# Which gate and up projections are made by seven products, and where their operand sums are traced

## The chip, the cores and the metric

The kernel runs on one core of one Trainium2 chip. The time is device microseconds from one execution of the whole program; the figure before is the median of three runs. TensorE multiplies, VectorE, ScalarE and GpSimd work elementwise, SyncE issues the transfers. In the profile's rows they are PE (PEld is its weight load), DVE, ACT, POOL and SP.

## The reference

Two layers of a decoder trunk over 512 tokens of width 1024, in f32. The part that the change touches is the feed-forward block of each layer:

```
hn = rms_norm(h, norm_ffn[i])
h = h + (jax.nn.silu(hn @ w_ffn_gate[i]) * (hn @ w_ffn_up[i])) @ w_ffn_down[i]
```

`w_ffn_gate` and `w_ffn_up` are 1024 x 2816, `w_ffn_down` 2816 x 1024. Ahead of the block stands the mixer (attention) with its output projection, behind it the layer's input embedding (`ple`), which begins with a norm of its own.

## The kernel before

Every f32 operand is cut into a high part, rounded to the matmul's format, and a low part, the rest; a product is then three matmuls (`mm3`: high x high, high x low, low x high). The cut of a weight tile is one ACT copy (`whl[:, 0]`) and one subtraction (`whl[:, 1]`) on POOL or DVE. There are five `whl` buffers, four `wraw` buffers for the raw weights as they land, and four `swtile` buffers `T`.

The norm (`norm_T`) runs over four tiles of 128 tokens. For each: ACT sums the squares (`junk`), POOL forms `msr`, `rsr` and the power, DVE scales two halves of the row (`xn`), PE transposes each half into a PSUM bank of tag "t" (two of them), ACT copies the high part to `xT`, DVE subtracts for the low part. In the feed-forward block ACT also copies the transposed half as it is to `xF`, for the operand sums.

The projections run over 11 pairs of column tiles, `fp` = 0 to 10. Pairs 0 to 5 are followed by the down projection of their part of `hidden`, then pairs 6 to 10 by the rest. In each pair the gate comes first (`wi` = 0), then the up projection (`wi` = 1). One of the two is done either

- plainly: 8 blocks of the contraction x 2 column tiles x 3 matmuls = 48 matmuls of 512 tokens into `gu`, with four weight tiles `whl`; or
- by seven products (`seven`), a scheme on 2 x 2 blocks of tokens, contraction and columns that needs seven block products instead of eight: 7 x 4 x 3 = 84 matmuls of 256 tokens into `st`, with seven `whl`, in the order 1, 7, 5, 2, 6, 4, 3. Products 1, 2 and 3 take raw blocks of the weights (low part on POOL); 7, 5, 6 and 4 take differences `T` that DVE forms (low part on DVE). Each product's result is then added into two output tiles `gs` by ACT and DVE.

On the token side products 1, 2 and 4 read `xT`; 7, 5, 6 and 3 read sums of its quarters (`Xw`, cut into `X`), which `operand_sums` makes once for each layer: four additions, four ACT copies, four subtractions of 1024 elements a partition. Before, pair 0 is plain, and in pairs 1 to 10 the gate goes by seven products and the up projection plainly. The operand sums are traced behind pair 0.

The order of the instructions on each engine is made by the tile scheduler: it goes by the order in which instructions are traced and by the offsets given with `prio` (`OFE` for evacuations, `OFN` for the norm, `KEEP` for the `xF` copies), and then each engine runs its list in that order.

Of the kernel before, what the change touches and what calls it, by code (L numbers as in the profile page):

```python
# [10 lines left out]
F32 = mybir.dt.float32  # L11
# [31 lines left out]
def hybrid_trunk_kernel(  # L43
# [18 lines left out]
    def f(ap):  # L62
        return ap.bitcast(F32)
# [43 lines left out]
    OFE, OFN, OFP = 100, 50, 200  # L107
    KEEP = 150

# [19 lines left out]
    @contextlib.contextmanager  # L129
    def prio(off):  # L130

        c = tc.cur_priority
        tc.cur_priority = c - off
        yield
        tc.cur_priority += off
# [236 lines left out]

    def norm_T(keep=None):


        g = next_gain.pop()
        xT = [[utile([P, 4, S], name=f"xT{i}{j}") for j in range(2)] for i in range(2)]
        with prio(OFN if last_act[0] else 5000):
            for tt, kh, xn in normed(g):
# [10 lines left out]
                latest["xT"] = ve.tensor_tensor(lo, pt, f(hi), op=ALU.subtract)  # L390
                if keep:
                    with prio(-KEEP):
                        se.activation(keep[kh][:, :, tt * P:(tt + 1) * P], pt, AF.Copy)

        def act(k, half, tt=None):
            t = xT[k // 4][half][:, k % 4, :]
            return t if tt is None else t[:, tt * P:(tt + 1) * P]
        return act

    def operand_sums(xact, F):  # L400


        a = [[F[kh][:, :, t * 256:(t + 1) * 256] for kh in range(2)] for t in range(2)]
        X = {}
        for n, (x, y, op) in ((7, (a[0][0], a[1][0], ALU.subtract)), (5, (a[1][0], a[1][1], ALU.add)),
                              (6, (5, a[0][0], ALU.subtract)), (3, (a[0][1], 6, ALU.subtract))):
            whole = utile([P, 4, 256], F32, name="Xw")
            F[n] = whole
            ve.tensor_tensor(whole, *(F[z] if isinstance(z, int) else z for z in (x, y)), op=op)
            X[n] = t = utile([P, 2, 4, 256], name=f"X{n}")  # L410
            se.activation(t[:, 0], whole, AF.Copy)  # L411
            ve.tensor_tensor(t[:, 1], whole, f(t[:, 0]), op=ALU.subtract)  # L412

        def left(n, half, k):
            if n in X:
                return X[n][:, half, k]
            t, kh = {1: (0, 0), 2: (0, 1), 4: (1, 1)}[n]
            return xact(4 * kh + k, half)[:, t * 256:(t + 1) * 256]
        return left
# [779 lines left out]
    def feed_forward(i, add_h, between):  # L1199
        lo_turn[0] = 2  # L1200
        F = dict(enumerate(utile([P, 4, S], F32, name=f"xF{j}") for j in range(2)))
        xact = norm_T(F)
        hidden, left = {}, None

# [3 lines left out]
        def units(fp):  # L1208
# [3 lines left out]
            def gate_done(j, t):  # L1212
                gate[j] = t
                se.activation(t, t, AF.Silu)

            def part(w, a2, ks, cols):
                for k, (hi, lo) in ks:
# [7 lines left out]
            for wi, w in enumerate((w_ffn_gate[i], w_ffn_up[i])):  # L1225
                if left and wi == 0:
                    seven(left, w, fp * 256, "ddss", gate_done)
                    continue
# [9 lines left out]
                else:  # L1238
                    part(w, accs, ws, slice(0, 512))
                if wi == 0:  # L1240
                    for j in range(2):
                        gate[j] = sg = etile("sg")
                        se.activation(sg, accs[j], AF.Silu)
            for j in range(2):
                sg = gate[j]
                ve.tensor_tensor(sg, sg, accs[j], op=ALU.mult)
                se.activation(hid[:, 0, j, :], sg, AF.Copy)
                ge.tensor_tensor(hid[:, 1, j, :], sg, f(hid[:, 0, j, :]), op=ALU.subtract)


        parts = range(0, 6), range(6, NF // 2)
        for fps in parts:
            for fp in fps:
                units(fp)
                if fp == 0:
                    left = operand_sums(xact, F)
            end = fps is parts[-1]
# [176 lines left out]
```

## Time and profile before

| | |
|---|---|
| median of three runs | 1566.41 us (1566.28, 1566.41, 1570.38) |
| the profiled execution's own time | 1570.22 us |
| its span, first to last instruction | 1568.4 us |
| PE busy | 1499.3 us, 96% of the span |
| DVE, ACT, POOL busy | 953.5, 800.1, 613.7 us |
| feed-forward pairs of layer 0 / layer 1 | from 356 us / from 1129 us of the span |

The rows further down come from one profiled execution. Times in them are from the start of its span; a row of the timeline has its start, its length, the engine, the line of the kernel, the operation, what it writes and reads, and in brackets the idle time of its engine just before it and who ended that. Matmuls are pipelined: the step from one start to the next is what one costs.

### The profile page before, as it was taken

To read this page: it belongs to the slowest core of one execution; us is meant where nothing else is said; L and a number is where in the kernel's file an instruction comes from. 1 tells how busy PE (TensorE), PEld (TensorE's weight loads), DVE (VectorE), ACT (ScalarE), POOL (GpSimd) and SP (SyncE) were. 2 spreads that over 40 slices of the span, in tenths; PEclk is the share of its full clock that TensorE was granted. 3 is DMA by queue.
4 is the path that set the end of the run, shared out by engine and by line. 5 is a ranking of instruction groups with operands and counts; after the bars stand their busy time and mean duration, and the time that the engine had idled before them with its cause. 6 is when DMAs were issued, how large, how long until landed. Compare 5 with 4: busy or idle time off the path is not lost.

```text
span 1568.4 us, 25192 instructions
## 1 busy us (share of the span) xinstructions
PE 1499.3 (96%) x9346; PEld 1307.9 (83%) x9346; DVE 953.5 (61%) x1840; ACT 800.1 (51%) x1705; POOL 613.7 (39%) x656
## 2 busy tenths in 40 slices
PE   6999999998999999999999999999889999999998
PEld 5898887877898888988988888778789888998888
DVE  6777869766763246534386878797666623654253
ACT  5476666655443234433355767586554432444343
POOL 3323455553344234432233235465434432444323
PEclk9999999999999999999999999999999999999999
DMA  5421321121333323342224131212223333334321
GB/s 174 124 73 42 82 68 34 48 94 58 104 95 99 99 85 108 108 134 68 81 69 123 55 80 44 81 28 64 71 81 95 94 121 95 94 95 132 111 68 54
DMA packets 114458, 134.70 MB, mean 86 GB/s; under 512 B 6864, under 2 KB 91936, under 8 KB 114336
## 3 DMA queue, kind: packets, MB, share of 16 engines
q1 hardware_dynamic: 114336, 133.10, 27.9%
q8 instruction: 74, 1.21, 0.3%
q14 instruction: 48, 0.39, 0.1%
HBM read 122.59 MB, written 2.10 MB: 80 GB/s over the span
## 4 chain that ended last, share of the span: by engine, by line
PE 76%; DVE 13%; ACT 4%; POOL 3%; issue 2%; DMA 1%; POOLq 0%; DVEq 0%; ACTq 0%; SPq 0%
PE acc L223 6%; PE acc L224 6%; PE acc L225 6%; PE gu L225 5%; PE gu L223 5%; PE gu L224 5%; PE st L224 4%; PE st L225 4%; PE st L223 4%; PE accr L223 2%; PE accr L224 2%; PE accr L225 2%; PE sc L866 2%; PE ge L223 2%; PE pTp L887 2%
## 5 line engine op out<-in xcount | busy, mean ns | idle before, releaser
L202 POOL TENSOR_TENSOR whl<-wraw,whl 128x512 fp32r<-128x512 f32 (+2 forms) x208 | 282.4, 1363 | 490.1 <-ACT whl L199 461.2
L199 ACT ACTIVATE whl<-wraw 128x512 fp32r<-128x512 f32 (+2 forms) x336 | 210.1, 631 | 263.6 <-PE acc L225 123.3
L202 DVE TENSOR_TENSOR whl<-wraw,whl 128x512 fp32r<-128x512 f32 x128 | 112.7, 882 | 171.7 <-ACT whl L199 171.3
L224 PE MATMUL gu<-xT,whl 128*128 128x512 f32 (+1 forms) x448 | 161.8, 362 | 0.0
L225 PE MATMUL gu<-xT,whl 128*128 128x512 f32 (+1 forms) x448 | 161.5, 362 | 0.0
L223 PE MATMUL gu<-xT,whl 128*128 128x512 f32 (+1 forms) x448 | 161.1, 361 | 0.0
L446 POOL TENSOR_TENSOR whl<-wraw,whl 128x512 fp32r<-128x512 f32 x60 | 87.1, 1452 | 153.7 <-ACT whl L445 153.6
L223 PE MATMUL acc<-whl,hid 128*128 128x512 f32 x352 | 139.1, 395 | 0.0
L224 PE MATMUL acc<-whl,hid 128*128 128x512 f32 x352 | 139.1, 395 | 0.0
L225 PE MATMUL acc<-whl,hid 128*128 128x512 f32 x352 | 138.8, 394 | 0.0
L446 DVE TENSOR_TENSOR whl<-T,whl 128x512 fp32r<-128x512 f32 x80 | 76.4, 955 | 66.2 <-ACT whl L445 65.6
L879 POOL TENSOR_SCALAR p<-p,rc,gt 128x128 f32<-128x128 f32 (+3 forms) x128 | 79.3, 630 | 71.0 <-DVE rc L877 20.8
L223 PE MATMUL st<-X,whl 128*128 128x256 f32 x320 | 91.5, 286 | 7.9 <-ACT X L411 7.9
L224 PE MATMUL st<-X,whl 128*128 128x256 f32 x320 | 92.1, 288 | 4.3 <-DVE X L412 4.3
L874 ACT ACTIVATE p<-sc,mx 128x128 f32<-128x128 f32 (+3 forms) x160 | 83.9, 535 | 22.7 <-DVE mx L871 20.6
L225 PEld LDWEIGHTS gu<-xT,whl 128*128 128x128 f32 x448 | 84.1, 188 | 13.5
L224 PEld LDWEIGHTS gu<-xT,whl 128*128 128x128 f32 x448 | 84.1, 188 | 13.0
L223 PEld LDWEIGHTS gu<-xT,whl 128*128 128x128 f32 x448 | 84.0, 188 | 12.9
L225 PE MATMUL st<-X,whl 128*128 128x256 f32 x320 | 91.4, 285 | 0.0
L445 ACT ACTIVATE whl<-T 128x512 fp32r<-128x512 f32 x80 | 50.1, 626 | 70.5 <-PE gu L225 57.4
L893 DVE TENSOR_TENSOR pT<-pTp,pT 128x512 fp32r<-128x512 f32 (+2 forms) x120 | 70.5, 596 | 19.5 <-ACT pT L892 18.5
L892 ACT ACTIVATE pT<-pTp 128x512 fp32r<-128x512 f32 (+2 forms) x120 | 62.1, 528 | 38.0 <-PE pTp L887 36.7
(334 smaller groups left out, 4499.4 us busy)
## 6 DMA issues: line engine op xcount, KB each, us to landing
wraw<-in_w_ffn_gate_dram SPq DMA_DIRECT2D x44, 512.0 KB, 3.6
wraw<-in_w_ffn_up_dram SPq DMA_DIRECT2D x44, 512.0 KB, 3.7
wraw<-in_w_ffn_down_dram SPq DMA_DIRECT2D x44, 512.0 KB, 3.8
wraw<-in_w_in_dram SPq DMA_DIRECT2D x36, 512.0 KB, 3.6
wraw<-in_w_out_dram SPq DMA_DIRECT2D x16, 512.0 KB, 3.8
wraw<-in_w_ple_gate_dram SPq DMA_DIRECT2D x16, 512.0 KB, 3.5
sw<-nq SPq DMA_DIRECT2D x32, 128.0 KB, 2.3
wraw<-in_w_in_dram SPq DMA_DIRECT2D x8, 280.0 KB, 2.9
```

The source lines that it names most:

```text
L199: se.activation(whl[:, 0], raw[:, lo:lo + n], AF.Copy)
L202: eng.tensor_tensor(whl[:, 1], raw[:, lo:lo + n], f(whl[:, 0]), op=ALU.subtract)
L223: i = te.matmul(acc, lhsT=lh, rhs=rh, start=start, stop=False, skip_group_check=True)
L224: te.matmul(acc, lhsT=lh, rhs=rl, start=False, stop=False, skip_group_check=True)
L225: te.matmul(acc, lhsT=ll, rhs=rh, start=False, stop=stop, skip_group_check=True)
L445: se.activation(whl[:, 0], src, AF.Copy)
L446: (ge if n in (1, 2, 3) else ve).tensor_tensor(whl[:, 1], src, f(whl[:, 0]), op=ALU.subtract)
L866: te.matmul(s[:, c:c + w], lhsT=lhsT, rhs=rhs, start=(j == 0), stop=False, skip_group_check=True)
L874: se.activation(e[:, u * n:(u + 1) * n], s[:, u * n:(u + 1) * n], AF.Exp, bias=mx[:, u:u + 1], accum_out=sm[:, u:u + 1])
L879: ge.tensor_scalar(e[:, u * n:(u + 1) * n], e[:, u * n:(u + 1) * n], rc[:, u:u + 1], gates[u] if gates else 1.0, op0=ALU.mult, op1=ALU.mult)
L892: se.activation(hi, src, AF.Copy)
L893: ve.tensor_tensor(lo, src, f(hi), op=ALU.subtract)
```

## The change

For `fp` of 1 or more, the projection with index `wi` goes by seven products where (2 fp + wi) is not a multiple of 3. So pair 1 has gate seven, up plain; pair 2 both seven; pair 3 gate plain, up seven; then the same again from pair 4. Of the 22 projections of a layer 13 go by seven products instead of 10. The steps behind an up projection (multiply, copy, subtract) become `up_done`, which an up projection by seven products calls for each of its two outputs.

The `xF` copies of ACT are gone. `operand_sums` adds the high and low parts of `xT` instead: two additions of 1024 elements on POOL (first 256 tokens) and two on DVE (last 256). It is traced between the gate and the up projection of pair 0.

```diff
--- before.py
+++ after.py
@@ -105,7 +105,6 @@
 
 
     OFE, OFN, OFP = 100, 50, 200
-    KEEP = 150
 
     def weave(*streams):
 
@@ -370,8 +369,7 @@
                 yield tt, kh, xn
         done.clear()
 
-    def norm_T(keep=None):
-
+    def norm_T():
 
         g = next_gain.pop()
         xT = [[utile([P, 4, S], name=f"xT{i}{j}") for j in range(2)] for i in range(2)]
@@ -388,28 +386,33 @@
                 if tt == 0 and kh == 1:
                     latest["first tile"] = last_act[0]
                 latest["xT"] = ve.tensor_tensor(lo, pt, f(hi), op=ALU.subtract)
-                if keep:
-                    with prio(-KEEP):
-                        se.activation(keep[kh][:, :, tt * P:(tt + 1) * P], pt, AF.Copy)
 
         def act(k, half, tt=None):
             t = xT[k // 4][half][:, k % 4, :]
             return t if tt is None else t[:, tt * P:(tt + 1) * P]
+        act.tiles = xT
         return act
 
-    def operand_sums(xact, F):
-
-
-        a = [[F[kh][:, :, t * 256:(t + 1) * 256] for kh in range(2)] for t in range(2)]
-        X = {}
-        for n, (x, y, op) in ((7, (a[0][0], a[1][0], ALU.subtract)), (5, (a[1][0], a[1][1], ALU.add)),
-                              (6, (5, a[0][0], ALU.subtract)), (3, (a[0][1], 6, ALU.subtract))):
-            whole = utile([P, 4, 256], F32, name="Xw")
-            F[n] = whole
-            ve.tensor_tensor(whole, *(F[z] if isinstance(z, int) else z for z in (x, y)), op=op)
-            X[n] = t = utile([P, 2, 4, 256], name=f"X{n}")
-            se.activation(t[:, 0], whole, AF.Copy)
-            ve.tensor_tensor(t[:, 1], whole, f(t[:, 0]), op=ALU.subtract)
+    def operand_sums(xact):
+
+
+        X, whole = {}, {}
+
+        for kh in range(2):
+            F = utile([P, 2, 4, 256], F32, name="xF")
+            for t in range(2):
+                hi, lo = (xact.tiles[kh][j][:, :, t * 256:(t + 1) * 256] for j in range(2))
+                whole[t, kh] = F[:, t]
+                (ve if t else ge).tensor_tensor(F[:, t], f(hi), f(lo), op=ALU.add)
+        for pair in (((7, (0, 0), (1, 0), ALU.subtract), (5, (1, 0), (1, 1), ALU.add)),
+                     ((6, 5, (0, 0), ALU.subtract), (3, (0, 1), 6, ALU.subtract))):
+            W = utile([P, 2, 4, 256], F32, name="Xw")
+            for j, (n, x, y, op) in enumerate(pair):
+                whole[n] = W[:, j]
+                ve.tensor_tensor(W[:, j], whole[x], whole[y], op=op)
+                X[n] = t = utile([P, 2, 4, 256], name=f"X{n}")
+                se.activation(t[:, 0], W[:, j], AF.Copy)
+                ve.tensor_tensor(t[:, 1], W[:, j], f(t[:, 0]), op=ALU.subtract)
 
         def left(n, half, k):
             if n in X:
@@ -1198,9 +1201,8 @@
 
     def feed_forward(i, add_h, between):
         lo_turn[0] = 2
-        F = dict(enumerate(utile([P, 4, S], F32, name=f"xF{j}") for j in range(2)))
-        xact = norm_T(F)
-        hidden, left = {}, None
+        xact = norm_T()
+        hidden, left = {}, []
 
         def hact(k, half, tt):
             return hidden[k // 2][:, half, k % 2, tt * P:(tt + 1) * P]
@@ -1212,6 +1214,12 @@
             def gate_done(j, t):
                 gate[j] = t
                 se.activation(t, t, AF.Silu)
+
+            def up_done(j, up):
+                sg = gate[j]
+                ve.tensor_tensor(sg, sg, up, op=ALU.mult)
+                se.activation(hid[:, 0, j, :], sg, AF.Copy)
+                ge.tensor_tensor(hid[:, 1, j, :], sg, f(hid[:, 0, j, :]), op=ALU.subtract)
 
             def part(w, a2, ks, cols):
                 for k, (hi, lo) in ks:
@@ -1223,8 +1231,9 @@
                             first.append(m.ins)
 
             for wi, w in enumerate((w_ffn_gate[i], w_ffn_up[i])):
-                if left and wi == 0:
-                    seven(left, w, fp * 256, "ddss", gate_done)
+
+                if fp and (2 * fp + wi) % 3:
+                    seven(left[0], w, fp * 256, ("ddss", "sott")[wi], (gate_done, up_done)[wi])
                     continue
                 accs = [bank(t, name=f"gu{wi}{j}") for j, t in enumerate(("dd", "ss" if fp == 0 else "to")[wi])]
                 ws = enumerate(weights(w, allk, fp * 256, 256, 2))
@@ -1237,23 +1246,20 @@
                         part(w, accs, ws, slice(256, 512))
                 else:
                     part(w, accs, ws, slice(0, 512))
-                if wi == 0:
-                    for j in range(2):
+                for j in range(2):
+                    if wi:
+                        up_done(j, accs[j])
+                    else:
                         gate[j] = sg = etile("sg")
                         se.activation(sg, accs[j], AF.Silu)
-            for j in range(2):
-                sg = gate[j]
-                ve.tensor_tensor(sg, sg, accs[j], op=ALU.mult)
-                se.activation(hid[:, 0, j, :], sg, AF.Copy)
-                ge.tensor_tensor(hid[:, 1, j, :], sg, f(hid[:, 0, j, :]), op=ALU.subtract)
+                if fp == 0 and wi == 0:
+                    left.append(operand_sums(xact))
 
 
         parts = range(0, 6), range(6, NF // 2)
         for fps in parts:
             for fp in fps:
                 units(fp)
-                if fp == 0:
-                    left = operand_sums(xact, F)
             end = fps is parts[-1]
             kts = list(range(2 * fps[0], 2 * fps[-1] + 2))
             for c, tags in ((0, "ddss"), (512, "stto")):
```

The rows that follow are the order of instructions on one engine, in layer 0; layer 1 has the same there. On POOL, around the norm of the feed-forward block, the kernel before has four times `msr`, `rsr` and power, one for each tile of tokens:

```order
L322 TENSOR_SCALAR msr<-ss 128x1
L335 TENSOR_TENSOR rsr<-msr,ss 128x1
L336 TENSOR_TENSOR rsr<-rsr,mhalf 128x1
L322 TENSOR_SCALAR msr<-ss 128x1
L335 TENSOR_TENSOR rsr<-msr,ss 128x1
L336 TENSOR_TENSOR rsr<-rsr,mhalf 128x1
L202 TENSOR_TENSOR whl<-wraw,whl 128x512 x2
```

These are the third and the fourth tile. In the changed kernel, same place (`xT_4407` and `xT_4408` are the high and low part of the first half of a row, `xT_4409` and `xT_4410` those of the second):

```order
L406 TENSOR_TENSOR xF<-xT_4407,xT_4408 128x1024
L321 TENSOR_SCALAR msr<-ss 128x1
L406 TENSOR_TENSOR xF<-xT_4409,xT_4410 128x1024
L334 TENSOR_TENSOR rsr<-msr,ss 128x1
L335 TENSOR_TENSOR rsr<-rsr,mhalf 128x1
L321 TENSOR_SCALAR msr<-ss 128x1
L334 TENSOR_TENSOR rsr<-msr,ss 128x1
L335 TENSOR_TENSOR rsr<-rsr,mhalf 128x1
L201 TENSOR_TENSOR whl<-wraw,whl 128x512 x2
```

Both of POOL's additions now stand ahead of the third tile's power.

On DVE, behind the last low part of `xT`, the kernel before goes on with weights, the multiplication of pair 0 (L1246) and only then the operand sums:

```order
L390 TENSOR_TENSOR xT_4412<-xnT,xT_4411 128x4x128
L202 TENSOR_TENSOR whl<-wraw,whl 128x512
L446 TENSOR_TENSOR whl<-T,whl 128x512 x2
L1246 TENSOR_TENSOR sg<-sg,gu_4632 128x512
L1246 TENSOR_TENSOR sg<-sg,gu_4633 128x512
L409 TENSOR_TENSOR Xw<-xF_4407 128x1024
L446 TENSOR_TENSOR whl<-T,whl 128x512
L409 TENSOR_TENSOR Xw<-xF_4407,xF_4408 128x1024
L462 TENSOR_TENSOR gs_4777<-part,st_4840 128x256
L412 TENSOR_TENSOR X_4754<-Xw,X_4754 128x1024
```

In the changed kernel, same place:

```order
L406 TENSOR_TENSOR xF<-xT_4407,xT_4408 128x1024
L406 TENSOR_TENSOR xF<-xT_4409,xT_4410 128x1024
L412 TENSOR_TENSOR Xw<-xF 128x1024 x2
L201 TENSOR_TENSOR whl<-wraw,whl 128x512
L415 TENSOR_TENSOR X_4630<-Xw,X_4630 128x1024
L434 TENSOR_TENSOR T<-wraw,T 128x512
L412 TENSOR_TENSOR Xw<-Xw,xF 128x1024
L415 TENSOR_TENSOR X_4634<-Xw,X_4634 128x1024
L412 TENSOR_TENSOR Xw<-xF,Xw 128x1024
L415 TENSOR_TENSOR X_4639<-Xw,X_4639 128x1024
L415 TENSOR_TENSOR X_4643<-Xw,X_4643 128x1024
L449 TENSOR_TENSOR whl<-T,whl 128x512 x2
```

All of the operand sums now stand ahead of the multiplication of pair 0 (L1220), which comes next.

On PE, 22 matmuls of pair 0 stand ahead of the third tile's transposes before; these are the last of them, the transposes, and what follows:

```order
L225 MATMUL gu_4514<-xT_4409,whl 128x256
L223 MATMUL gu_4515<-xT_4409,whl 128x256
L382 MATMUL xnT<-ident,xn 128x128 x4
L224 MATMUL gu_4515<-xT_4410,whl 128x256
L225 MATMUL gu_4515<-xT_4409,whl 128x256
```

In the changed kernel 28 of them stand ahead of these transposes, and the tile's second transposes follow one matmul later:

```order
L224 MATMUL gu_4504<-xT_4409,whl 128x256
L222 MATMUL gu_4505<-xT_4409,whl 128x256
L380 MATMUL xnT<-ident,xn 128x128 x4
L223 MATMUL gu_4505<-xT_4410,whl 128x256
L380 MATMUL xnT<-ident,xn 128x128 x4
```

Before the fourth tile's last transposes PE has 51 matmuls of pair 0 behind it in the old order, and 43 in the new. In the new order DVE also scales both halves of the third and of the fourth tile (four `xn`) ahead of the third tile's low parts.

## Rows read from the trace of the kernel before

**Rows 1.** The profile page, busy time of each engine, share, instructions

```profile
PE 1499.3 (96%) x9346; PEld 1307.9 (83%) x9346; DVE 953.5 (61%) x1840; ACT 800.1 (51%) x1705; POOL 613.7 (39%) x656
```

**Rows 2.** Busy time in four stretches: start, end, length; engines; clock, DMA

```profile
core 0: us, PE busy (x) PEld busy (x) DVE busy (x) ACT busy (x) POOL busy (x), PEclk, DMA share, GB/s
382.96:413.14 30.18, 24.18 (x134) 21.10 (x133) 24.29 (x26) 13.53 (x22) 12.80 (x8) 0.89 0.26 79
413.14:423.03 9.89, 9.89 (x85) 9.88 (x84) 6.20 (x9) 6.17 (x12) 6.05 (x5) 1.00 0.24 72
423.03:434.11 11.08, 11.08 (x51) 9.02 (x49) 7.05 (x10) 3.57 (x6) 3.90 (x3) 1.00 0.40 126
1155.75:1185.35 29.60, 23.42 (x135) 20.41 (x134) 24.59 (x26) 13.53 (x22) 12.52 (x8) 0.94 0.27 81
```

**Rows 3.** Timeline of PE: where pairs begin and where it waits for sums

```profile
382.96 0.28 PE L223 MATMUL st<-xT,whl 128*128 128x256 f32 x1
...
390.27 0.58 PE L223 MATMUL st<-X,whl 128*128 128x256 f32 x1 [3.21 <-ACT X L411]
...
400.20 0.39 PE L224 MATMUL st<-X,whl 128*128 128x256 f32 x1 [1.51 <-DVE X L412]
...
413.14 0.28 PE L223 MATMUL st<-xT,whl 128*128 128x256 f32 x1
```

**Rows 4.** Timeline of PE: transposes of the third and the fourth tile

```profile
359.81 0.63 PE L382 MATMUL xnT<-ident,xn 128*128 128x128 f32 x4 [0.81 <-DVE xn L369]
...
364.02 0.63 PE L382 MATMUL xnT<-ident,xn 128*128 128x128 f32 x4 [0.90 <-DVE xn L369]
...
365.83 0.66 PE L382 MATMUL xnT<-ident,xn 128*128 128x128 f32 x4
```

**Rows 5.** Timeline of POOL and DVE, same stretch of the norm

```profile
356.32 0.22 POOL L322 TENSOR_SCALAR msr<-ss 128x1 f32<-128x1 f32 x1 [3.55 <-ACT junk L313]
358.05 0.19 POOL L335 TENSOR_TENSOR rsr<-msr,ss 128x1 f32<-128x1 f32 x1 [1.51 <-ACT junk L313]
358.31 0.57 POOL L336 TENSOR_TENSOR rsr<-rsr,mhalf 128x1 f32<-128x1 f32 x1
...
355.33 0.68 DVE L390 TENSOR_TENSOR xT<-xnT,xT 128x512 fp32r<-128x512 f32 x1
...
358.92 0.75 DVE L369 SCALAR_TENSOR_TENSOR xn<-h,rsr,gx 128x512 f32<-128x512 f32 x1 [0.80 <-POOL rsr L336]
```

**Rows 6.** Line L202: POOL at 1024 elements, ns least/median/most

```profile
L202 POOL TENSOR_TENSOR we<-wraw,we x2: 2398/2401/2404, 679.4 to 1451.3; 128x1024 fp32r<-128x1024 f32 x2
```

**Rows 7.** Granted clock of PE (third from last) after two gaps

```profile
1016.00:1020.00 4.00, 1.68 (x10) 1.17 (x10) 4.00 (x12) 3.69 (x17) 0.35 (x1) 1.00 0.13 49
...
246.00:247.00 1.00, 1.00 (x5) 0.73 (x4) 1.00 (x6) 1.00 (x4) 1.00 (x3) 0.50 0.00 0
```

**Rows 8.** Timeline of PE: the ends of those two gaps

```profile
244.53 0.44 PE L866 MATMUL sc<-nk,nq 128*128 128x384 f32 x1 [2.30 <-ACT p L874]
...
1018.38 0.44 PE L866 MATMUL sc<-nk,nq 128*128 128x384 f32 x1 [2.32 <-ACT p L874]
```

**Rows 9.** Timeline of DVE: one operand sum alone

```profile
392.41 1.21 DVE L409 TENSOR_TENSOR Xw<-Xw,xF 128x1024 f32<-128x1024 f32 x1
```

**Rows 10.** Timeline of POOL and DVE within the seven products of pair 2

```profile
414.62 2.54 POOL L1248 TENSOR_TENSOR hid<-gs,hid 128x512 fp32r<-128x512 f32 x2 [1.98 <-ACT hid L1247]
417.15 1.72 POOL L446 TENSOR_TENSOR whl<-wraw,whl 128x512 fp32r<-128x512 f32 x1
...
414.06 0.69 DVE L446 TENSOR_TENSOR whl<-T,whl 128x512 fp32r<-128x512 f32 x1
415.89 1.83 DVE L446 TENSOR_TENSOR whl<-T,whl 128x512 fp32r<-128x512 f32 x1 [1.14 <-ACT whl L445]
417.65 0.42 DVE L460 TENSOR_TENSOR part<-part,st 128x256 f32<-128x256 f32 x1
```

## The prediction, made before the changed kernel ran

> **What bounds the kernel now.** I read the page's busy times first: PE works 96% of the span, the next engine, DVE, 61% [rows 1]. An average hides stages, so the windows came next, cut where a gate's first `st` matmul or an up projection's first `gu` matmul starts. In the settled part of the feed-forward block PE never waits: pair 2 takes 9.89 us for the gate by seven products and 11.08 us for the plain up projection, 20.97 together, at full clock [rows 2]. There only fewer or cheaper matmuls shorten anything. Pair 1 is different: the same work takes 30.18 us in layer 0 and 29.60 us in layer 1 [rows 2]. The timeline shows why: PE waits 3.21 us for the cut of an operand sum and 1.51 us for another, the largest of several waits [rows 3], DVE is busy 24.29 of 30.18 us, and the clock averages 0.89 [rows 2], since it falls to half behind the long wait. The sums are formed only behind pair 0's multiplication, when PE already wants them. Last I looked at the norm ahead of pair 0, where the change puts work on POOL: there PE waits 0.81 and 0.90 us for scaled rows [rows 4], and these wait for POOL's power (0.57 us, [rows 5]).
>
> **Six projections more by seven products.** Three more for each layer. One saves 11.08 - 9.89 = 1.19 us of PE [rows 2], if PE stays the bound: 6 x 1.19 = **7.1 us**.
>
> **Sums ahead of need.** Pair 1 loses 30.18 - 20.97 = 9.2 us in layer 0 and 29.60 - 20.97 = 8.6 us in layer 1 [rows 2], half clock included: **17.8 us**, if the sums come in time. DVE has now ten operations of 1.21 us [rows 9] (two additions for `xF`, four sums, four low parts) and four of 0.69 us [rows 10] up to the low part of pair 1's second `T`, 14.9 us. POOL's three operations on `whl` meanwhile take turns with them (see the lock below) at an estimated 1.3 us each (2.54 us for two, [rows 10]): 18.7 us. By the norm's walk below DVE starts at about 369.0, so that low part is there at 387.7 and the one before it at 387.0. PE ends pair 0 at 382.96 [rows 3] plus the norm's 2.1 us, 385.1, and a product lasts 9.89 / 7 = 1.41 us, so product 7 wants its low part at about 386.7. I put 0.4 us for each layer on it, **0.8 us**; the ends are 0 and half of the old loss, 4.5 us for each layer.
>
> **The norm's power waits behind POOL's additions.** Of 1024 elements one such operation takes POOL 2.40 us [rows 6]. The first is ready when DVE has written the second tile's first low part, 355.33 + 0.68 = 356.0 [rows 5]; it ends at 358.4; `msr` (0.22) follows; the second addition lasts to 361.0; then `rsr` (0.19) and the power (0.57) [rows 5], with some 0.1 us between them, end at 362.0. Before they ended at 358.9, so `xn` starts 3.1 us later. PE has six more matmuls of 0.12 us (9.89 / 84, [rows 2]) to do ahead of these transposes, but then waits some 3.2 us instead of 0.81. The fourth tile catches up in part: its power ends at about 364.1, DVE scales four halves until 365.6 and then writes two low parts, which free the two PSUM banks for the fourth tile's transposes, the last of them at about 367.0 instead of 365.83 [rows 4], with 43 matmuls of pair 0 done instead of 51. That is 1.2 + 8 x 0.12 = 2.1 us for each layer. A PE wait of this length can also halve the clock: behind a wait of 2.30 us [rows 8] PE ran at 0.50, the 1.2 GHz level [rows 7], for some 3.7 us, which costs half of that, 1.85 us; behind 2.32 us [rows 8] it kept 1.00 [rows 7]; behind 3.21 us [rows 3] it fell. Two of three: 1.2 us. Together 3.3 us for each layer, **6.6 us**; the ends are 0 (the additions are over before anyone asks) and 4.0 for each layer. The Trainium skill ("TensorE: Matmul & The Clock Gate", Part 1) has half rate as the state of an idle array, released by activity; by it each of the two waits would cost the whole 1.85 us, and the sum would be 1.3 us worse. One wait in rows 8 kept the clock, so I don't take it whole.
>
> ACT loses its eight `xF` copies for each layer. Two of them stand in the norm's chain, but that chain now goes through POOL, so this counts nothing.
>
> **Two projections by seven products in a row.** The twelve new neighbours: in each layer six times two such projections follow each other (pair 2; 3 and 4; 5; 6 and 7; 8; 9 and 10). PE needs 2 x 9.89 = 19.8 us for two. DVE's operations on two SBUF operands and POOL's exclude each other: the low part at 415.89 took 1.83 us instead of 0.69 and ended 0.6 us after POOL's operation that was under way, while the addition at 417.65, which reads PSUM, took its 0.42 us beside POOL [rows 10]. In two neighbours these are 16 x 0.69 on DVE and 8 x 1.3 on POOL (six low parts, one pair's two `hid`), 21.4 us, and 1.4 more where an up projection's outputs, now in SBUF, are multiplied: 1.6 to 3.0 us more than PE needs. The plain projections between have 4.0 to 8.0 us of such work in 11.08, so the average holds and only the lead counts. Five `whl` buffers let the cut run ahead: product 4 of pair 2 had its low part at 415.89 + 1.83 = 417.7 [rows 10], and PE came to it at 413.14 + 5 x 1.41 + two matmuls = 420.4, a lead of 2.7 us. So most of the excess is covered; I take 0.15 us for each of 12 places, **1.8 us**, with ends 0 and 3.0. The Trainium skill ("SBUF — State Buffer", Who interferes with whom) states the same lock, an operation of DVE with two SBUF inputs against one of POOL that reads SBUF, the later one blocked for the whole of the other; it speaks against this change, and it is the second rival below.
>
> **No cost.** ACT would be at some 14 us in 19.8 (6.17 in 9.89 with one such projection, [rows 2]) and stays short of PE. The `ple` loads move on SP from pair 0 to pair 10; their transposes stay where they were, in the last pair, and have them by then. Raw weights for a second projection in a row land during the plain one ahead of it.
>
> **Sum.** 7.1 + 17.8 - 0.8 - 6.6 - 1.8 = 15.7 us. The profiled execution's own time is 1570.22 us (span 1568.4 and 1.8 around it), so it would be 1554.5. It lies 3.8 us above the median of the three runs, of which one reads 1570.38 and two 1566.3 to 1566.4; I take the difference from the median: 1566.4 - 15.7 = **1550.7 us**, with its own range of 1546 to 1557.
>
> **Rivals.**
> First, POOL's additions cost nothing, because they are over before the third tile's sum of squares is there. For it: POOL idles 3.55 us there [rows 5]. Against: both stand ahead of the power on POOL. It gives 6.6 us more, 1544.1.
> Second, the lock becomes the bound in the twelve places, and the kernel gets slower. DVE's list is in order; an addition that waits for PE holds up the differences behind it, so the lead may not build up. Without this stall the gain is 17.5 us, so from 1.46 us for each place the gain is gone. At 2.5 us each, 30 instead of 1.8, it is 1578.9.
> Third, the change doesn't do what it says: the sums are traced early but still come late, since DVE's 18.7 us fit with nothing to spare. With half the old loss left (8.9 instead of 0.8) it is 1558.8.
>
> **How the numbers follow.** A measurement here can tell about 0.3%, 4.7 us, from no change: faster is below 1561.7, slower above 1571.1. My forecast has 0.57, the first rival 0.12, the third 0.12, the second 0.10 (a third of it between 1562 and 1571), and 0.09 is for what I don't see, a third of it on each side and between. Faster 0.57 + 0.12 + 0.12 + 0.03 = 0.84, same 0.03 + 0.03 = 0.06, slower 0.10. The range has to hold 0.8: forecast, first and third rival make 0.81, from 1541.5 (nothing lost of 24.9) to 1561.
>
> **What would show it.** Pair 1 of both layers, from its first `st` matmul to that of pair 2, should take some 21.4 us instead of 30.18 and 29.60. In the norm POOL should show two additions of about 2.4 us ahead of the third tile's power, and PE one wait of about 3.2 us for `xn`. Pairs 2, 5 and 8 should take 19.8 us each with no wait of PE; waits on `whl` there for DVE's or POOL's low part would be the second rival. The prediction is wrong if PE's waits in the feed-forward block together exceed some 10 us, or if a projection by seven products takes more than 10 us behind another.

## The result, and the profile after

The kernel after takes 1551.16 us (median of 5 runs, 1549.74 to 1553.40), the kernel before 1570.23 (median of 5, 1566.28 to 1572.16): a ratio of 0.9883, 95% interval 0.9863 to 0.9904, some 19 us faster. The forecast was 1550.7, in a range of 1541.5 to 1561. The profiled execution has a span of 1548.0 us against 1568.4. Busy times of the page after, to be read beside [rows 1]:

```profile
PE 1490.1 (96%) x9562; PEld 1313.8 (85%) x9562; DVE 1004.0 (65%) x1910; ACT 809.3 (52%) x1725; POOL 650.3 (42%) x666
```

PE has 216 matmuls more and is busy 9 us less, and its share is the same 96%. Where the time went is read from stretches cut where a pair's first matmul starts, as in [rows 2]. In this order: pair 0, pair 1 and the two neighbouring projections by seven of pair 2 (all layer 0), then pairs 0 and 1 of layer 1.

```profile
core 0: us, PE busy (x) PEld busy (x) DVE busy (x) ACT busy (x) POOL busy (x), PEclk, DMA share, GB/s
355.47:384.35 28.88, 25.15 (x209) 24.59 (x208) 24.37 (x26) 15.16 (x25) 12.98 (x11) 1.00 0.18 56
384.35:405.48 21.13, 21.13 (x135) 19.00 (x134) 14.74 (x22) 9.81 (x19) 11.59 (x8) 1.00 0.33 100
405.48:425.26 19.78, 19.78 (x170) 19.78 (x168) 14.47 (x21) 12.42 (x24) 10.88 (x8) 1.00 0.29 89
1117.42:1147.15 29.73, 26.45 (x210) 26.06 (x208) 24.39 (x26) 15.19 (x26) 12.93 (x11) 0.94 0.17 54
1147.15:1168.30 21.15, 21.15 (x135) 19.03 (x134) 14.72 (x22) 9.81 (x19) 11.66 (x8) 1.00 0.33 100
```

Pair 1 takes 21.13 and 21.15 us with PE busy throughout; it took 30.18 and 29.60 [rows 2]. Two projections by seven in a row take 19.78 us, twice 9.89. Of the pairs only pair 0 got longer: it took 26.72 and 26.68 us and takes 28.88 and 29.73. The view of waits says how, for PE from the start of pair 0 to the end of pair 10, layer 0 and layer 1 (columns: who waited for whom, us in total, times, longest):

```profile
PE xnT L380 <- DVE xn L368: 3.2, 1, 3.2
PE xnT L380 <- DVE xT L388: 0.5, 1, 0.5
...
PE xnT L380 <- DVE xn L368: 3.3, 1, 3.3
```

The view shows no other wait of PE there. None is for a sum or for a cut weight. The timeline of POOL, then of DVE, around the long wait of layer 0, against [rows 5]:

```profile
355.33 2.42 POOL L406 TENSOR_TENSOR xF<-xT,xT 128x1024 f32<-128x1024 f32 x1 [3.33 <-DVE xT L388]
357.83 0.22 POOL L321 TENSOR_SCALAR msr<-ss 128x1 f32<-128x1 f32 x1
358.13 2.36 POOL L406 TENSOR_TENSOR xF<-xT,xT 128x1024 f32<-128x1024 f32 x1
360.45 0.19 POOL L334 TENSOR_TENSOR rsr<-msr,ss 128x1 f32<-128x1 f32 x1
360.72 0.57 POOL L335 TENSOR_TENSOR rsr<-rsr,mhalf 128x1 f32<-128x1 f32 x1
...
361.32 1.41 DVE L368 SCALAR_TENSOR_TENSOR xn<-h,rsr,gx 128x512 f32<-128x512 f32 x2 [3.45 <-POOL rsr L335]
```

The power, at 358.31 before, is now at 360.72, though the whole stretch lies 0.8 us earlier in this profile; it stands behind two additions of some 2.4 us. DVE is idle for 3.45 us waiting for it, and PE waits behind DVE. From first gate matmul to the end of the second down projection, the two layers get 10.3 and 8.8 us shorter, 19.1 together; the other 1.3 of the 20.4 us by which the span shrank lie outside these blocks.

### The profile page after: what moved, and what is told of

Same layout as the page of the kernel before. It is cut to its first block, busy times and chain, and to the rows that moved or that the text cites. A ratio compares the mean times of both kernels' runs of the same rounds, so it can differ in the third digit from the quotient of the medians.

```text
span 1548.0 us, 25774 instructions
## 1 busy us (share of the span) xinstructions
PE 1490.1 (96%) x9562; PEld 1313.8 (85%) x9562; DVE 1004.0 (65%) x1910; ACT 809.3 (52%) x1725; POOL 650.3 (42%) x666
## 4 chain that ended last, share of the span: by engine, by line
PE 78%; DVE 11%; POOL 4%; ACT 3%; issue 2%; DMA 0%; POOLq 0%; ACTq 0%; DVEq 0%
PE acc L222 6%; PE acc L223 6%; PE acc L224 6%; PE st L223 6%; PE st L222 6%; PE st L224 6%; PE gu L223 4%; PE gu L224 4%; PE gu L222 4%; PE accr L222 2%; PE accr L223 2%; PE sc L869 2%; PE accr L224 2%; PE no L1086 2%; PE pTp L890 2%
## 5 line engine op out<-in xcount | busy, mean ns | idle before, releaser
L201 POOL TENSOR_TENSOR whl<-wraw,whl 128x512 fp32r<-128x512 f32 (+2 forms) x196 | 270.0, 1384 | 467.1 <-ACT whl L198 453.7
L198 ACT ACTIVATE whl<-wraw 128x512 fp32r<-128x512 f32 (+2 forms) x312 | 195.1, 631 | 254.4 <-PE acc L224 136.8
L201 DVE TENSOR_TENSOR whl<-wraw,whl 128x512 fp32r<-128x512 f32 x116 | 103.1, 891 | 171.6 <-ACT whl L198 171.3
L449 POOL TENSOR_TENSOR whl<-wraw,whl 128x512 fp32r<-128x512 f32 x78 | 116.1, 1496 | 141.5 <-ACT whl L448 139.2
L223 PE MATMUL gu<-xT,whl 128*128 128x512 f32 (+1 forms) x352 | 124.8, 355 | 0.0
L224 PE MATMUL gu<-xT,whl 128*128 128x512 f32 (+1 forms) x352 | 124.6, 355 | 0.0
L222 PE MATMUL gu<-xT,whl 128*128 128x512 f32 (+1 forms) x352 | 124.0, 354 | 0.0
L449 DVE TENSOR_TENSOR whl<-T,whl 128x512 fp32r<-128x512 f32 x104 | 102.6, 993 | 29.3 <-ACT whl L448 28.9
L223 PE MATMUL st<-X,whl 128*128 128x256 f32 x416 | 116.9, 281 | 0.0
L222 PE MATMUL st<-X,whl 128*128 128x256 f32 x416 | 116.8, 281 | 0.0
L224 PE MATMUL st<-X,whl 128*128 128x256 f32 x416 | 116.6, 280 | 0.0
L223 PE MATMUL st<-xT,whl 128*128 128x256 f32 x312 | 87.6, 281 | 0.0
L224 PE MATMUL st<-xT,whl 128*128 128x256 f32 x312 | 87.5, 280 | 0.0
L222 PE MATMUL st<-xT,whl 128*128 128x256 f32 x312 | 87.5, 280 | 0.0
L448 ACT ACTIVATE whl<-T 128x512 fp32r<-128x512 f32 x104 | 64.2, 625 | 42.8 <-PE gu L224 24.2
L896 DVE TENSOR_TENSOR pT<-pTp,pT 128x512 fp32r<-128x512 f32 (+2 forms) x120 | 70.5, 595 | 19.9 <-ACT pT L895 18.9
```

Source lines behind the costliest of these rows:

```text
L198: se.activation(whl[:, 0], raw[:, lo:lo + n], AF.Copy)
L201: eng.tensor_tensor(whl[:, 1], raw[:, lo:lo + n], f(whl[:, 0]), op=ALU.subtract)
L222: i = te.matmul(acc, lhsT=lh, rhs=rh, start=start, stop=False, skip_group_check=True)
L223: te.matmul(acc, lhsT=lh, rhs=rl, start=False, stop=False, skip_group_check=True)
L224: te.matmul(acc, lhsT=ll, rhs=rh, start=False, stop=stop, skip_group_check=True)
L448: se.activation(whl[:, 0], src, AF.Copy)
```

## Experiments

Each is the kernel after with the edit shown; e1 to e10 are short names. The kernel before ran beside them: 1571.4 us with e1 to e4, 1572.2 with e5 to e8 and 1571.2 with the last three. The figures in brackets behind a median are the lowest and the highest run, the ratio to the kernel before and its 95% interval. From the end of layer 0's feed-forward block to layer 1's pair 0 two profiles of one kernel stand up to 2.7 us apart (405.4 us in e6 and 402.7 in e9, the same kernel), so the verdicts rest on the lengths of single stretches first, and on the medians second.

**The sums without the new rule (e2).**

```diff
-                if fp and (2 * fp + wi) % 3:
+                if fp and wi == 0:
```

> The changed kernel with the old rule: gate by seven products in every pair from 1 on, up always plainly; only the place of the operand sums is new. Theory (the two parts add): 6 x 1.19 = 7.1 us more than the changed kernel, 1558.3, pair 1 at 21.1 us, every later pair at 20.97, pair 0 still at 28.9 and 29.7. Rival (the six more projections by seven products bring nothing, and all of the gain is in the place of the sums): 1551.

It took 1557.4 us (1555.1 to 1559.7; 0.9908, 0.9889 to 0.9927). Pair 1 takes 21.17 and 21.08 us, pair 0 28.82 and 30.64, and pairs 2 to 9 some 21.0 each. So some 14 us of the gain come from the early sums alone, net of the longer pair 0. The rule brings the rest: 5 to 6 us by the medians, and by the lengths of pairs 2 to 10, which are 3.5 and 3.6 us shorter in the kernel after, the 7.1 that six conversions make at 1.19 us. The 30.64 is longer than any pair 0 forecast here; the clock stands at half for 6.8 us of it (see the account of the norm below).

**The rule without the early sums (e3).**

```diff
-                if fp == 0 and wi == 0:
+                if fp == 0 and wi == 1:
```

> The changed kernel with the operand sums traced behind pair 0, as before, and the new rule for the projections. Theory: pair 1 takes some 30 us again (9 us more in each layer), pair 0 gets its 26.7 us back since POOL's additions no longer stand ahead of the power; in all 17.5 - 5.2 = 12 us more than the changed kernel, 1563.5. Rival (the place of the sums doesn't matter, since the sums are now made by DVE and POOL from the cut parts and not from ACT's copies): pair 1 stays near 21 us, 1551 or less.

It took 1575.4 us (1571.0 to 1579.2; 1.0026, 1.0014 to 1.0038), slightly slower than before, where I had expected 1563.5. Pair 0 goes to 25.88 and 26.15 us: the long wait there does come from the place of the additions. But pair 1 takes 36.8 and 36.6 us, some seven more than before. Timeline of POOL, then DVE, in pair 1:

```profile
381.55 2.40 POOL L406 TENSOR_TENSOR xF<-xT,xT 128x1024 f32<-128x1024 f32 x1
383.90 4.45 POOL L1222 TENSOR_TENSOR hid<-sg,hid 128x512 fp32r<-128x512 f32 x2
388.31 3.33 POOL L406 TENSOR_TENSOR xF<-xT,xT 128x1024 f32<-128x1024 f32 x1
...
381.84 5.38 DVE L406 TENSOR_TENSOR xF<-xT,xT 128x1024 f32<-128x1024 f32 x2
...
387.48 5.24 DVE L412 TENSOR_TENSOR Xw<-xF 128x1024 f32<-128x1024 f32 x2
```

Both engines now add side by side, each operation waiting for one of the other engine's: DVE's two additions take 5.38 us (2.35 in the kernel after) and its first two sums 5.24. PE's waits in pair 1 grow from 6.0 us before to 12.0, and the clock is at half for 13.7 us in either layer instead of 6.8 and 3.4; what share of the seven us is the clock's is not shown. Splitting the four additions over DVE and POOL saves nothing when both halves are wanted at once.

**POOL's additions behind the fourth tile's power (e1).**

```diff
-                (ve if t else ge).tensor_tensor(F[:, t], f(hi), f(lo), op=ALU.add)
+                if t:
+                    ve.tensor_tensor(F[:, t], f(hi), f(lo), op=ALU.add)
+                else:
+                    with tc.issue_after(latest["pow"].ins):
+                        ge.tensor_tensor(F[:, t], f(hi), f(lo), op=ALU.add)
```

> The changed kernel, with POOL's two additions of the operand sums held back until the fourth tile's power has been issued. Theory (the additions stand ahead of the power on POOL and so delay the norm): PE's wait of 3.2 us for xn goes, pair 0 takes 26.7 to 27.2 us again instead of 28.9 and 29.7, pair 1 stays at 21.1 because POOL is idle behind the power and DVE wants the sums only some 2 us later; about 5 us less than the changed kernel, 1546. Rival (the wait has another cause, the order of the sums of squares or of the matmuls): pair 0 stays at 29 us and the time at 1551.

It took 1556.6 us (1553.8 to 1558.9; 0.9902, 0.9884 to 0.992), and pair 0 grew to 31.14 and 32.27 us instead of shrinking. The power is early now, but look at POOL, and at DVE just after it:

```profile
364.63 0.57 POOL L335 TENSOR_TENSOR rsr<-rsr,mhalf 128x1 f32<-128x1 f32 x1
365.16 5.10 POOL L410 TENSOR_TENSOR xF<-xT,xT 128x1024 f32<-128x1024 f32 x2
...
365.23 5.58 DVE L368 SCALAR_TENSOR_TENSOR xn<-h,rsr,gx 128x512 f32<-128x512 f32 x2 [0.38 <-POOL rsr L335]
```

DVE's two scaled rows of the fourth tile, 1.41 us elsewhere, take 5.58: each comes behind one of POOL's additions, since they read two SBUF operands too. PE waits 2.52 and 2.01 us for them, and from the second wait on the clock is at half for 3.4 us in layer 0 and 6.8 in layer 1. My expectation moved the additions out of POOL's queue for the power and put them under the lock that the prediction itself had named. In the kernel after, the same additions run while DVE is idle or reads PSUM, so there the queue costs, and here the lock.

**No additions on POOL, in two ways (e7 and e6).** First all four on DVE, e7:

```diff
-                (ve if t else ge).tensor_tensor(F[:, t], f(hi), f(lo), op=ALU.add)
+                ve.tensor_tensor(F[:, t], f(hi), f(lo), op=ALU.add)
```

> The kernel after with all four additions on DVE, none on POOL. Theory (it is POOL's place ahead of the power that costs, and DVE has no room to spare before pair 1): pair 0 goes back to 26.7 to 27.7 us, but DVE carries 2.4 us more before product 7 of pair 1 while pair 1 begins some 2 us earlier, so pair 1 grows from 21.1 to 22 to 23.5 us, with a PE wait on an operand sum or a low part; the median is 1547 to 1551. Rival (the sums had room): pair 0 at 26.7 and pair 1 at 21.1, 1546. Rival (the lock between DVE and POOL has no part in it and the place ahead of the power costs nothing): pair 0 stays at 28.9 to 29.7.

Then none at all, e6, with the whole activations copied out of PSUM by ACT as in the kernel before (only the main lines are shown; the helper's additions drop out, `whole[t, kh]` is a view of `kept[kh]`):

```diff
+                if keep:
+                    with prio(-150):
+                        se.activation(keep[kh][:, tt // 2, :, tt % 2 * P:tt % 2 * P + P], pt, AF.Copy)
...
-                (ve if t else ge).tensor_tensor(F[:, t], f(hi), f(lo), op=ALU.add)
```

> The kernel after, but the four whole activations are written by ScalarE's eight copies out of PSUM, as in the kernel before, and the four additions (two on POOL, two on DVE) are gone; the sums are still traced early. Theory (POOL's additions ahead of the third tile's power make pair 0 of each layer longer): pair 0 takes 26.7 us again in both layers instead of 28.88 and 29.73, the PE wait of 3.24 and 3.28 us for scaled rows goes back to some 0.8, pair 1 stays at 21.0 (DVE has 2.4 us less to do), and the median is 1551.2 - 5.2 = 1546 us. Rival (the longer pair 0 comes from the sums of the early tracing on DVE, or the eight ACT copies cost as much where they now stand): pair 0 stays at 28.5 or more and the median at 1550 to 1553.

With the copies it took 1547.8 us (1543.2 to 1549.8; 0.9843, 0.9824 to 0.9862). Pair 0 is back at 26.72 and 26.80 us, PE's waits there are 0.83 and 0.91 (0.85 and 0.89), and pair 1 takes 20.96 and 20.99. So of all that is now traced early it is the additions that cost in the norm.

With everything on DVE it took 1551.7 us (1549.0 to 1554.1; 0.9872, 0.9856 to 0.9887), just above the range I gave and for a reason I had not foreseen: pair 1 takes 20.96 us, and pair 0 stays long, 29.84 and 30.06. PE's long wait for `xn` is gone (0.32 and 0.24 us are left), so that one was POOL's doing; but now PE waits for POOL itself. PE, POOL and DVE in that kernel:

```profile
371.01 0.58 PE L224 MATMUL gu<-xT,whl 128*128 128x256 f32 x1 [2.64 <-POOL whl L201]
...
364.64 8.03 POOL L201 TENSOR_TENSOR whl<-wraw,whl 128x512 fp32r<-128x512 f32 x2 [5.50 <-ACT whl L198]
...
362.84 2.35 DVE L406 TENSOR_TENSOR xF<-xT,xT 128x1024 f32<-128x1024 f32 x2
365.11 2.35 DVE L412 TENSOR_TENSOR Xw<-xF 128x1024 f32<-128x1024 f32 x2
367.38 0.68 DVE L201 TENSOR_TENSOR whl<-wraw,whl 128x512 fp32r<-128x512 f32 x1
367.98 1.22 DVE L415 TENSOR_TENSOR X<-Xw,X 128x1024 fp32r<-128x1024 f32 x1
```

DVE issues operations on two SBUF operands without a gap, each starting as the last one ends, and two cuts on POOL, some 1.3 us each elsewhere, take 8.03. The first alone takes 6.32: it waits through six operations of DVE (from the second `xF` to a `T` behind the rows shown) and ends behind the first pause in that row. The second takes 1.77. A loser of the lock does not always wait that long: in the kernel after two such cuts, under a row of DVE just as dense, take 1.79 and 2.35 us, so each got its turn behind one operation. What decides between the two is not shown. From PE's wait of 2.64 us on the clock is at half for 3.4 us in both layers, which is part of the longer pair 0. (Counted from the norm's first transposes, which the mixer puts 4.4 us earlier in layer 0 of this profile, pair 1 begins 3.1 and 3.3 us later than with the copies.)

**All projections of pairs 1 to 10 by seven (e4, and e8 with more load buffers).**

```diff
-                if fp and (2 * fp + wi) % 3:
+                if fp:
```

> The changed kernel with both projections of every pair from 1 on by seven products, 20 in a layer instead of 13, with no plain one between. Theory (the exclusion of DVE and POOL is the bound where no plain projection lets the lead be rebuilt): a pair takes 21.4 to 22.8 us, the sum of DVE's operations on two SBUF operands and POOL's, instead of 19.8, with PE waiting for low parts of the weights; 20 pairs at 22.1 come to some 29 us more than the changed kernel, 1580, and not below 1565. Rival (the exclusion costs nothing, PE stays the bound): pairs at 19.8 us, 14 x 1.19 = 16.7 us less than the changed kernel, 1534.5.

It took 1605.6 us (1604.3 to 1609.0; 1.0218, 1.0201 to 1.0235). A pair takes 23.8 us on average in the first half of the block and 22.7 in the second; behind the first pairs of a half it settles at some 23.8 in both, more than the 21.4 to 22.8 which I worked out for the lock, so something else was in it. DVE's waits between 395 and 490 us:

```profile
DVE T L434 <- DMA wraw<-in_w_ffn_up_dram: 12.2, 4, 3.4
DVE T L434 <- DMA wraw<-in_w_ffn_gate_dram: 10.3, 4, 3.4
DVE whl L449 <- ACT whl L448: 1.1, 4, 0.3
```

DVE waits 22.5 us for raw weights. There are four buffers of them, two for each projection by seven, and SP's queue waits for POOL to let one go: the third projection in a row loads late. So the next run, e8, gave it six buffers, and 14 instead of 15 large tiles to make room.

```diff
-        raw = wpool.tile([P, 1024], F32, name="wraw", tag="wraw", bufs=4)
+        raw = wpool.tile([P, 1024], F32, name="wraw", tag="wraw", bufs=6)
```

> All projections of pairs 1 to 10 by seven products, as in e4_all_seven, but with six buffers for raw weights instead of four (and 14 instead of 15 large tiles, to make room). Theory A (in e4_all_seven DVE waited 22.5 us for raw weights between 395 and 490 us, since SP's queue waits for a raw buffer that POOL still reads; three projections by seven in a row use up the lead of the loads): a pair takes 20 us or little more instead of 23.8 and 22.7, and the median is about 1536 to 1545 us. Theory B (the lock between DVE and POOL is the bound: 21.4 us of operations that exclude each other, and 22.8 with the multiplications on SBUF operands, against 19.8 of PE): a pair stays at 21.4 to 22.8 us with PE waiting for low parts, and the median is 1580 to 1600.

It took 1576.7 us (1572.3 to 1577.9; 1.0024, 1.0012 to 1.0035); with fewer large tiles its pair 0 takes 32.1 us, so only its later pairs are compared. Each half of either layer takes 105.0 to 105.4 us for five pairs, 21.0 for one on average. That average hides the lead: the first pair of a half takes 19.8 us and the second 19.9 to 20.4, and only from the third on does a pair settle, at some 21.6 (21.6 to 22.1). The third pair of layer 0, in the columns of [rows 2]:

```profile
435.75:457.36 21.61, 20.64 (x170) 20.06 (x169) 21.15 (x29) 11.74 (x24) 12.81 (x8) 1.00 0.33 98
```

DVE's waits for loads are gone and DVE is busy 21.15 of 21.61 us, its blocked time included: now it is the bound. So theory A explains some 2.2 us of e4's loss for each settled pair, and theory B the last 1.8. Both causes were in e4. Theory B's pair, 21.4 to 22.8 us, came out in the settled pairs; neither median did, and the longer pair 0 blurs that comparison. DVE's operations start 0.60 us apart though each row gives 0.68 or 0.69: with the two multiplications by the gate that is 18 x 0.60 + 8 x 1.3 = 21.2, an estimate in which the additions that read PSUM run beside POOL.

**One buffer of cut weights less (e5).**

```diff
-        whl = wpool.tile([P, 2, 560], F32R, name="whl", tag="whl", bufs=5)[:, :, :n]
+        whl = wpool.tile([P, 2, 560], F32R, name="whl", tag="whl", bufs=4)[:, :, :n]
```

(and the same in the helper for seven products; that line is not shown)

> The kernel after with four buffers of cut weights (whl) instead of five. My prediction covered the excess of two projections by seven in a row (21.4 to 22.8 us of DVE and POOL work against 19.8 of PE) by the lead that five buffers give, some 2.7 us. If that lead is what covers it, one buffer less takes 1.4 us of it: PE then waits in the back-to-back places of pairs 2, 3 to 4, 5, 6 to 7, 8 and 9 to 10, up to 1.4 us each, 12 places: 1556 to 1568 us. If the lead is not needed (the excess is not there, or the plain projection between carries it), nothing changes: 1551, with pair 2 at 19.8.

It took 1567.6 us (1564.8 to 1572.0; 0.9974, 0.9962 to 0.9985), within the range I gave for a needed lead, but that time says nothing on it: 16 us came from the stages that also cut weights, the mixers and pair 0 (30.90 and 31.32). In the places themselves pair 2 takes 20.12 instead of 19.78 us and pairs 3 and 4 19.90 instead of 19.81; the twelve places lose 2.6 us together, 0.05 to 0.36 each. So the fifth buffer's lead is used, but for little.

**The copies again beside the kernel after (e9), and three of four by seven (e10).** The first two runs are the kernel after unchanged and, as e9, the kernel of e6, on one chip.

> The kernel after, unchanged, beside the next two on one chip: 1551 us, pair 0 at 28.9 and 28.9 to 29.7 us.

> The same kernel as e6_act_copies, beside the kernel after on one chip. By the segments of its trace (pair 0 2.16 and 2.93 us shorter, pair 1 0.17 and 0.16) it should be 5.4 us faster than after, 1546 us; by the medians of two different chips the difference was only 3.4 us. If it is under 2 us, part of the gain is given back somewhere that the two profiles don't show.

They took 1550.2 us (1548.3 to 1553.9; 0.9866, 0.9848 to 0.9885) and 1546.9 (1542.6 to 1549.2; 0.9838, 0.9816 to 0.986): 3.3 us apart, where the feed-forward blocks of the two profiles differ by 5.6. The two intervals overlap, so the size of the gain is open between the two numbers. Then e10, the copies with three of four projections by seven:

```diff
-                if fp and (2 * fp + wi) % 3:
+                if fp and (2 * fp + wi) % 4 != 3:
```

> e6_act_copies with three of four projections by seven products in place of two of three (plain are only the up projections of pairs 1, 3, 5, 7, 9): two conversions more for each layer, 4 x 1.19 = 4.8 us less PE. Theory (the lead covers the excess of three in a row, 1.8 us at the 21.0 us for two that e8_all_seven_raw6 needed when all were by seven products): three in a row take 29.7 us, and the median is 4.8 us under e9's, about 1541. Rival (four buffers of raw weights hold only two projections by seven, so that the third loads late, as in e4_all_seven): the third takes 0.5 to 2 us more in 8 places of the two layers, PE waits there for low parts whose difference on DVE waited for a load, and the median is equal to e9's or up to 11 us above.

It took 1544.3 us (1543.6 to 1546.2; 0.9827, 0.9809 to 0.9845), the lowest median of all, 5.9 us under the kernel after beside it; its interval overlaps that of e9. Three in a row:

```profile
405.82:435.50 29.68, 29.68 (x253) 29.67 (x252) 26.84 (x34) 17.96 (x36) 19.30 (x12) 1.00 0.28 80
```

That is 3 x 9.89 without a stall, in all eight places (29.68 to 29.74), though DVE waits three times for loads in layer 0's first half, up to 2.5 us; the rival is out. At e8's settled rate three in a row would want an estimated 32.4 us, 2.7 more than PE and not the 1.8 of my expectation; that is as much as the lead of 2.7 that the prediction read from [rows 10]. But the gain on e9 is 2.6 us and not 4.8. Pairs 6 to 10, where the two conversions of a layer lie, are 2.11 and 2.01 us shorter instead of 2.38, and the second down projection behind them is 0.75 and 0.81 longer: PE idles 0.74 and 0.75 us there ahead of a transpose of `ple`, and has no such idle time in e9. By these stretches it is 2.6.

## Why the prediction was right, and where it was not

**The conversions** (7.1 us): pairs 2 to 10 are 3.44 us shorter in layer 0 and 3.66 in layer 1, 7.1.

**The sums** (17.8 less 0.8): pair 1 is 9.05 and 8.45 us shorter, 17.5. The low parts were in time to within 0.2 us (pair 1's gate takes 10.05 and 10.06 us instead of 9.89), where I had 0.4 for each layer. Timeline of DVE:

```profile
381.75 2.43 DVE L415 TENSOR_TENSOR X<-Xw,X 128x1024 fp32r<-128x1024 f32 x2
384.09 2.39 DVE L449 TENSOR_TENSOR whl<-T,whl 128x512 fp32r<-128x512 f32 x2
```

The second `T`'s low part ends at 386.5; I had said 387.7. Of these 1.2 us, 0.8 is only that the stretch lies that much earlier in this profile. DVE needs 18.4 us for the row, from 368.1 on, where I had 18.7, and two errors of mine cancel in that: an operation that is not blocked costs 1.13 us from start to start (0.60 for 512 elements), where I took its row's 1.21 (0.69), so the fourteen cost 13.7 us and not 14.9; and POOL's cuts, four and not three, hold DVE up for 4.7 us and not 3.9. The third rival (sums still late) fell here.

**The norm** (6.6): 2.16 and 3.05, 5.2. The mechanism, the place and the wait (3.24 and 3.28 us, some 3.2 forecast) came out, and 2.1 us without the clock was right: 2.16. The mis-sized term is the clock. In layer 0 PE kept the full clock behind the wait; in layer 1 the clock fell to half, 1.2 GHz, for 3.4 us; a stretch of one us within it, and pair 0 of e2's layer 1, where the same norm stands, in the columns of [rows 2] (the granted clock is third from last):

```profile
1126.00:1127.00 1.00, 1.00 (x6) 1.00 (x6) 1.00 (x3) 0.14 (x1) 0.00 (x0) 0.50 0.00 0
...
1121.05:1151.69 30.64, 27.36 (x209) 27.12 (x208) 24.34 (x26) 15.14 (x25) 12.95 (x11) 0.89 0.20 61
```

I had 1.85 us for a fall, half of some 3.7 us at the low clock; the stretch of [rows 7] from which I took them lasts 3.4. Here a fall cost 0.85 (29.73 - 28.88), and in the second profile of the same kernel 0.89 (29.72 in layer 0, where it fell, and 28.83 in layer 1, where it did not). Where the clock holds, PE reaches the fourth tile's transposes early and idles 0.48 us for them (the second wait above); where it falls, that wait is not there. Part of the half clock is thus spent in time that PE would have waited anyway; the rest of the difference is not explained. The price is not fixed: in e2, with the same wait, the clock held in layer 0 (pair 0 28.82 us) and stood at half for 6.8 us in layer 1 (30.64), 1.82 us, about what I had for one fall. With the two layers of e4 (29.51 and 30.67, both fallen) that makes eight waits of 3.23 to 3.28 us in the same norm, of which five cost the clock; two of three was a fair chance. The Trainium skill ("TensorE: Matmul & The Clock Gate", Part 1) has half rate as the state of an idle array. The traces agree in that each of these falls comes with a long wait; the prediction's reading, that by it each wait costs the clock, went too far, for three of the eight did not. The first rival (additions free) fell.

**Neighbours by seven** (1.8): nothing; all twelve places take 19.77 to 19.84 us. The excess itself was sized rightly: the settled rate under the lock is 21.6 (e8), 1.8 above PE's, within my 1.6 to 3.0. The lead covers it wholly, where I had left 0.15 us for each place, and the plain projection between gives it back. So the second rival's mechanism exists, but not even three in a row (e10) reach it, with four buffers of raw weights. The rule in the Trainium skill ("SBUF — State Buffer", Who interferes with whom), that the loser is blocked for the whole of the other's instruction, agrees with e1 and e3, where each operation waits for one of the other engine's (DVE's scaled rows take 2.8 us each behind POOL's additions of 2.3 and 2.8); in e7 a cut waits through six.

**ACT's copies** (0): not shown for the kernel after, since no run has both the copies and POOL's early additions. Where the additions are out of the way the copies do cost: with neither (e3) pair 0 takes 25.88 and 26.15 us, with the copies (e6) 26.72 and 26.80. Of the other things taken as free, the transposes of `ple` did stay where they were and PE does not wait for them, though only two of the eight stand in the last pair and six in the down projection behind it.

**The basis.** The terms come to 15.7 us, and the two layers gained 19.1: the norm and the neighbours were 3.2 too dear, the sums came to 0.5 more than forecast, and 0.3 is lost in the second down projection of layer 1 (59.34 us instead of 59.04), which I had not counted. That 1550.7 met 1551.2 so closely is chance: I took the difference from a median of three runs, 1566.4, and two more runs moved that median to 1570.2. Against the profiled execution, which the sum was made from, it would have been 1554.5.

**Open.** Why the clock falls behind one of these waits and not behind another (3.24 us did it in e4 and not in the kernel after); what decides whether POOL gets its turn behind one operation of DVE or behind six; and how much of e9's 5.6 us shows in the time.

## What to carry to other kernels

When work moves to an idle engine, ask what stands behind it in that engine's queue, and which of another engine's operations it locks out; here either way cost more than leaving the copies on ACT, which reads PSUM and stood in neither's way (e6). A resource with little excess (21.6 us wanted, 19.8 given) does no harm as long as the buffers hold its lead and something cheap comes in between; when a stall is bigger than the excess, as in e4, look for a second cause, such as the turn of the load buffers.

## What the runs showed of the hardware

Operations of DVE that are ready start 0.60 us apart at 512 elements and 1.13 at 1024, where their rows give 0.68 and 1.21. Under an unbroken row of DVE operations on two SBUF operands POOL got one cut of 1.3 us done in 6.32 us (e7), and others in 1.79 and 2.35 (the kernel after); under two POOL additions DVE's two scaled rows took 5.58 instead of 1.41 (e1). Two projections by seven products, with their 18 such operations on DVE and 8 on POOL, sustained 21.6 us (e8). A wait of some 3.25 us halved TensorE's clock in five of eight cases of the same code, with no difference that the profile shows; pair 0 was 0.7 to 0.9 us longer where the clock stayed low for 3.4 us, and 1.8 where it did for 6.8.
